# A gating mixer's two dense products by seven block products for eight

## The chip, the cores and the metric

One core of one Trainium2 chip runs the whole program: matrix engine (PE, with its weight loads PEld), vector engine (DVE), scalar engine (ACT), GpSimd (POOL) and the DMA queues, here issued by SP. The metric is the device time of one launch in microseconds, as the median of several runs.

## The reference

Two decoder layers on 1024 positions of width 1024, in float32. Layer 0 mixes tokens by a gating unit, layer 1 by dilated attention; each is followed by a squared-ReLU MLP of width 4096, with RMS norms in front and plain residual adds. The part that is changed:

```python
def _chunk_gating_mixer(h, w_in, ln_g, ln_b, w_s, b_s, w_out):
    uv = jax.nn.gelu(h @ w_in, approximate=False)
    u, v = jnp.split(uv, 2, axis=-1)
    v = _layer_norm(v, ln_g, ln_b)
    v = v.reshape(B_, nc, CHUNK, GATE_GROUPS, GATE_GROUP_DIM)
    w = jnp.where(causal[None], w_s, 0.0)
    mixed = jnp.einsum('gts,bnsgc->bntgc', w, v) + b_s.T[None, None, :, :, None]
    gate = mixed.reshape(B_, S_, GATE_WIDTH)
    return (u * gate) @ w_out
```

with `h = x + mixer(rms_norm(x))`. So there are three dense products here, v, u and the output, each 1024 x 1024 x 1024, and a small causal product inside each chunk of 128 positions.

## The kernel before

Activations lie transposed, channels on the partitions: `h` is eight tiles of 128 channels by 1024 positions, worked on in two halves of 512. A float32 product is made of three passes: every operand is split into a high part (ACT copies it into a rounded type, L208) and a low part (DVE subtracts, L209), and PE does high x high, high x low and low x high. So a block of 128 x 128 weights with 512 columns is three matmuls, and each weight tile costs one ACT and one DVE operation for each 512 columns (`split`, `weight`, `Pair`).

PE's instructions stand in the order in which the program writes them. `Flow` keeps a rough PE clock by which side work (norms, the gate, attention) is woven into that order. The other engines' orders come from a scheduler that ranks by the order of writing and by `tc.high_priority`. An engine takes its queue strictly in order. Tiles come from pools: `wpool` with 8 weight tiles, `slots` with 28 large tiles, `tpool` with 8 temporaries `t`, 4 raw weight tiles `r` and 2 spares `b`; PSUM has 3 banks `mm` and 5 banks `at`. A new tile waits for whoever still uses its buffer.

The mixer runs in this order:

1. The v product, eight chunks of 128 positions in groups of three, three and two (`gi` = 0, 1, 2), over eight depth blocks k; each k needs one split weight pair from `w_v`. While it runs, x is scaled by the norm's gain and split (`scaled`, L456 and L457), and its squares are summed on POOL (`Square`, L264). The RMS factor is applied later: to v in the gelu (L538), to u by `rsb`.
2. `spatial`, woven in for each chunk: statistics, normalising (L511), split, 24 small matmuls against the causal gate weights, and the gate back to SBUF (L525) in place of v in `vg`.
3. The u product, output tile by output tile (`mm`, 24 matmuls for each half), then `u_out`: times `rsb` (L589), gelu (L590), times the gate (L593), and `u_split`.
4. The output product in the same plain form, added to `h` by `add_h` (L308).

The MLPs already use block products by seven (the scheme of Strassen and Winograd): both operands are cut into 2 x 2 blocks, sums of blocks are formed, and seven products give what eight gave. `Weights` loads four raw blocks and `steps` forms the sums on POOL (L351 to L356) and splits the seven operands; `product` runs one of them; `Terms` forms the sums of the normed input; `hidden_terms` those of the hidden activations, which are stored in DRAM and fetched again. `Down` is the MLP's second product: it goes in turns over the depth blocks, adds each product to `h` where it belongs (L830), and keeps the last depth block (`we`, `xe`) as a plain product for the end (`close`), so that the next norm can start by halves.

Of the kernel before, what the change touches and what calls it, by code (L numbers as in the profile page):

```python
# [10 lines left out]
F32 = mybir.dt.float32  # L11
# [101 lines left out]
def trunk(ctx: ExitStack, tc: tile.TileContext, xT, w_u, w_v, w_o, w_s, b_s, w_qkv, w_vt, w_bo, rel,  # L113
# [5 lines left out]
    slots = ctx.enter_context(tc.tile_pool(name="slots", bufs=28))  # L119
    wpool = ctx.enter_context(tc.tile_pool(name="wpool", bufs=8))  # L120
    tpool = ctx.enter_context(tc.tile_pool(name="tpool", bufs=8))
    small = ctx.enter_context(tc.tile_pool(name="small", bufs=4))
# [18 lines left out]
    class Pair:  # L141


        def __init__(self, t):
            self.hi, self.lo = t[:, 0, :], t[:, 1, :]

        def split(self, src):
            n = src.shape[1]
            split(self.hi[:, 0:n], self.lo[:, 0:n], src)
            return self  # L150
# [49 lines left out]
    h = [const.tile([P, S], F32, name=f"h{k}") for k in range(KT)]  # L200
# [6 lines left out]
    def split(hi, lo, src):  # L207
        nc.scalar.activation(hi, src, AF.Copy)  # L208
        nc.vector.tensor_tensor(lo, src, hi.bitcast(F32), op=ALU.subtract)  # L209
# [116 lines left out]
    def product(bank, w, xs, more=False):  # L326

        for k, x in enumerate(xs):
            three(bank, w, blk(k), x, not more and k == 0, k == len(xs) - 1, skip_group_check=True)
            flow.pump()  # L330

    class Weights:
# [10 lines left out]
        def split(self, p, src):  # L343
            self.w[p] = self.place().split(src)
# [104 lines left out]
    def scaled(s, k):  # L449

        x, g = h[k][:, half(s)], vec[:, 0, k:k + 1]
        hi, lo = pair().both()
# [5 lines left out]
        ys[s].append((hi, lo))  # L458
        sq[s].add(k)

# [36 lines left out]
    def spatial():  # L497
        for n in range(8):
            yield v_done[n], 600
            v = vg[n]  # L500
            st = small.tile([P, 2, 6], F32, tag="bn", name="bn")
# [6 lines left out]
            for i in range(2):  # L508
                t, hi, lo = temp(), rtemp(), rtemp()
                c = slice(i * HALF, (i + 1) * HALF)  # L510
                nc.vector.tensor_scalar(t, v[:, c], mv[:, 0:1], r, op0=ALU.subtract, op1=ALU.mult)  # L511
                split(hi, lo, t)
                parts.append((hi, lo))
            yield LAT["gate"]
# [15 lines left out]
    gelus = []  # L530
# [11 lines left out]
    for gi, chunks in enumerate(((0, 1, 2), (3, 4, 5), (6, 7))):  # L542
        banks = {}
        for k in range(KT):
# [7 lines left out]
            with tc.issue_after(roots[0] if k == 1 else gelus[5]) if gi == 1 and k else nullcontext():  # L552
                w = weight(w_v[k])
# [20 lines left out]
            for e, i, n, f in order:  # L574
                x, c = ys[n // 4][k], blk(n % 4)
# [4 lines left out]
                if k == 7 and e == 2 and f == 1:  # L580
# [3 lines left out]
                    else:  # L584
                        v_out(banks, chunks[:i + 1])

    def u_out(m, s, ps):
        t = temp()
        nc.vector.tensor_tensor(t, ps, rsb[:, half(s)], op=ALU.mult)  # L589
        nc.scalar.activation(t, t, AF.Gelu)  # L590
        for b in range(4):
            x = vg[4 * s + b][:, blk(m)]
            nc.vector.tensor_tensor(x, x, t[:, blk(b)], op=ALU.mult)  # L593

    def u_split(s):
        out = []
        for m in range(8):
            hi, lo = pair().both()
            for b in range(4):
                split(hi[:, blk(b)], lo[:, blk(b)], vg[4 * s + b][:, blk(m)])  # L600
            out.append((hi, lo))
        return out

    us = []
    for tiles in ((0, 1, 2), (3,), (4,), (5, 6, 7)):
        w = [weight(w_u[m]) for m in tiles]
        for s in range(2):
            for i, m in enumerate(tiles):
                b = mm_bank()
                mm(b, w[i], KCOLS, ys[s])  # L610
                flow.until(lambda: gated[4 * s + 3].t is not None)
                u_out(m, s, b)
            if tiles[-1] == 7:
                us.append(u_split(s))


    sq = [Square(half(0)), Square(half(1))]
    terms = Terms()
    for tiles in ((0, 1), (2,), (3,), (4, 5, 6, 7)):
        w = [weight(w_o[m]) for m in tiles]  # L620
        for s in range(2):
            for i, m in enumerate(tiles):
                b = mm_bank()
                mm(b, w[i], KCOLS, us[s])
                add_h(m, half(s), b)
                sq[s].add(m)
            if tiles[-1] == 7:
                start_terms(sq[s], s, 1, terms)
                if s == 0:
                    first = [plain(0, q) for q in range(2)]  # L630

# [17 lines left out]
    def hidden_terms(q, c11, c21, c12, c22, t2, store=True):  # L649
# [11 lines left out]
        return {1: c11, 3: c22, 7: t3, 5: c12, 2: c21, 6: t2, 4: t4}  # L661

    def mlp(layer, x, first, last):
# [35 lines left out]
        for q in range(2, 16):  # L699
            down = Down(layer) if q == 15 else None  # L700
# [74 lines left out]
    class Down:  # L775

        def __init__(self, layer):
            self.layer = layer
            self.order = [14, *range(14)]
            self.x = {k: {} for k in self.order}
            self.u = {}
            self.todo = [(t % 4, range(max(0, t - 3), min(t, 14) + 1)) for t in range(18)]

        def weights(self, t, **kw):
            a, ks = self.todo[t]

            runs = []
            for k in (self.order[i] for i in ks):
                if runs and k == runs[-1][1]:
                    runs[-1][1] += 1
                else:
                    runs.append([k, k + 1])
            return Weights(lambda i, j: [w_dn[self.layer, a, i, j][:, lo * P:hi * P] for lo, hi in runs], **kw)

        def take(self, k, src, which):
            for p in which:  # L800
                self.x[k][p] = pair("hx").split(src[p])

        def early(self, which):

            src = {}
            for n, p in enumerate(which):
                if n % 2 == 0:
                    two = slot((P, 2, HALF), F32, "hr")
                src[p] = load(hidden_tile(0, p), two[:, n % 2, :])
            self.take(0, src, which)  # L810

        def inputs(self, t, which):
            k = self.order[t] if t < 15 else 0
            if k:
                self.take(k, {p: load(hidden_tile(k, p), temp()) for p in which}, which)

        def run(self, w):
            for t, (a, ks) in enumerate(self.todo):
                hs = {(i, s): h[a + 4 * i][:, half(s)] for i in range(2) for s in range(2)}
                wn = None  # L820
                if t < 17:
                    wn = self.weights(t + 1, **(dict(own=temp, place=pair) if t == 16 else {}))
                more = ahead(wn)
                more()

                def xs(p):
                    return [self.x[self.order[k]][p] for k in ks]

                def add(i, s, src, engine=nc.vector):
                    return engine.tensor_tensor(hs[i, s], hs[i, s], src, op=ALU.add).ins  # L830

                def then(evacuated, p):

                    with tc.issue_after(evacuated) if t < 3 else nullcontext():
                        more()
                        self.inputs(t + 1, (p,))

                if t == 16:
                    self.ends(0)
                a_ = mm_bank()  # L840
                product(a_, w[1], xs(1))
                if t < 4:
                    self.u[a] = spare() if t < 2 else temp()
                    more()
                    nc.scalar.activation(self.u[a], a_, AF.Copy)
                    self.inputs(t + 1, (1,))
                else:
                    more()
                    nc.vector.tensor_tensor(self.u[a], self.u[a], a_, op=ALU.add)
                    self.inputs(t + 1, (1,))  # L850
                d = at_bank()
                product(d, w[5], xs(5))
                then(add(1, 1, d), 5)
                e = at_bank()
                product(e, w[7], xs(7))
                then(add(1, 1, e), 7)
                if t == 16:
                    self.ends(1)
                b = at_bank()
                product(b, w[6], xs(6))  # L860
                then(nc.vector.tensor_tensor(self.u[a], self.u[a], b, op=ALU.add).ins, 6)
                product(a_, w[2], xs(2), True)
                then(add(0, 0, a_), 2)
                product(d, w[3], xs(3), True)
                then(add(0, 1, d), 3)
                if t >= 14:
# [624 lines left out]
```

## Time and profile before

| | |
|---|---|
| runs | 2171.8 us median of 3 (2170.54 to 2172.2) |
| profiled execution | span 2174.9 us |
| PE busy | 2139.6 us (98%) |
| DVE busy | 1541.6 us (71%) |
| ACT busy | 1086.5 us (50%) |
| POOL busy | 514.3 us (24%) |
| DMA | 253.88 MB, mean 117 GB/s |
| granted PE clock | 0.996 |

The span is that of one profiled execution, and the page has no other time for it. An engine's busy time is the sum of its instructions' durations; a row of a timeline has the start, the duration, the engine, the line, the operation, what it writes and reads, the shape and, in brackets, how long the engine had been idle in front of it and who ended that. Start-to-start times of instructions that follow each other are a little shorter than their durations, since they overlap at the ends.

### The profile page before, as it was taken

Reading aid. Unit: us, or ns where it says so; the run is one execution under the profiler, and the core shown is the slowest. Engines: PE = TensorE matmul, PEld = TensorE weight load, DVE = VectorE, ACT = ScalarE, POOL = GpSimd, SP = SyncE. Lnnn points to the kernel's source line nnn. Section 1 sums busy time; section 2 is a strip of 40 time slices with the busy share of each in tenths; the row PEclk is TensorE's granted clock in tenths of the full one; section 3 lists DMA queues with packets and bytes.
Section 4 is the critical chain, followed back from the end, with each engine's and each line's share of the span. In section 5 each row is a group of like instructions: output and inputs, shape, how many; then the busy total and the mean of one; then the engine's idle time right before and its main releaser. Section 6 shows DMA issues by size and latency. Waiting matters only on the chain.

```text
span 2174.9 us, 30386 instructions
## 1 busy us (share of the span) xinstructions
PE 2139.6 (98%) x10360; PEld 1774.5 (82%) x10360; DVE 1541.6 (71%) x2855; ACT 1086.5 (50%) x2200; POOL 514.3 (24%) x372
## 2 busy tenths in 40 slices
PE   9999999999999999999999999999999999999997
PEld 7888887888878888788888887887788888788886
DVE  7865277766689887771357676758986667988867
ACT  7644145555564443351356464656555556544433
POOL 2000124333234323510000000001443332333335
PEclk9999999999999999999999999999999999999999
DMA  6421104444355443333321222221155443654432
GB/s 214 131 73 49 39 22 166 160 158 150 119 183 186 146 149 107 107 119 135 121 72 58 74 65 55 75 55 30 39 179 160 156 152 118 193 168 145 151 92 97
DMA packets 167680, 253.88 MB, mean 117 GB/s; under 512 B 33642, under 2 KB 59365, under 8 KB 167525
## 3 DMA queue, kind: packets, MB, share of 16 engines
q1 hardware_dynamic: 166768, 250.71, 36.4%
q8 instruction: 81, 1.33, 0.3%
q10 hardware_dynamic: 756, 1.23, 0.2%
q14 instruction: 75, 0.61, 0.1%
HBM read 182.50 MB, written 69.37 MB: 116 GB/s over the span
## 4 chain that ended last, share of the span: by engine, by line
PE 80%; DVE 8%; DMA 5%; ACT 4%; issue 2%; POOL 1%; SPq 1%; DVEq 0%; ACTq 0%; POOLq 0%
PE at L180 40%; PE mm L180 39%; PE at L187 1%; DMA t<-bvec 1%; ACT t L1136 1%; DVE wp L209 1%; DMA sc<-st 1%; DMA h<-in_xT 1%; DMA r<-in_w_dn 1%; DMA t<-in_w_dl 1%; DVE N L1174 1%; DMA hr<-hid 1%; DVE h L308 0%; DVE h L830 0%; DVE wlo L209 0%
## 5 line engine op out<-in xcount | busy, mean ns | idle before, releaser
L208 ACT ACTIVATE wp<-r 128x512 fp32r<-128x512 f32 (+2 forms) x404 | 240.9, 600 | 356.4 <-PE at L180 229.0
L180 PE MATMUL at<-hx,wp 128*128 128x512 f32 x1770 | 412.9, 389 | 1.7 <-DVE h L830 1.7
L180 PE MATMUL mm<-y,whi 128*128 128x512 f32 x1312 | 412.4, 395 | 0.0
L180 PEld LDWEIGHTS at<-hx,wp 128*128 128x128 f32 x1770 | 332.0, 188 | 71.7 <-DVE h L830 2.6
L209 DVE TENSOR_TENSOR wp<-r,wp 128x512 fp32r<-128x512 f32 (+2 forms) x404 | 323.5, 808 | 77.2 <-ACT wp L208 73.7
L180 PE MATMUL at<-t,wp 128*128 128x512 f32 x1344 | 313.9, 389 | 0.0
L180 PEld LDWEIGHTS at<-t,wp 128*128 128x128 f32 x1344 | 252.2, 188 | 52.8 <-DVE t L739 0.4
L264 POOL TENSOR_TENSOR t<-t 128x512 f32<-128x512 f32 (+1 forms) x66 | 84.1, 1274 | 860.6 <-ACT t L259 858.4
L180 PEld LDWEIGHTS mm<-y,whi 128*128 128x128 f32 x1312 | 240.7, 188 | 50.6
L180 PE MATMUL mm<-y,wlo 128*128 128x512 f32 x656 | 256.0, 390 | 0.0
L351 POOL TENSOR_TENSOR t<-r 128x512 f32<-128x512 f32 (+3 forms) x62 | 92.7, 1494 | 596.6 <-DMA r<-in_w_up 194.1
L180 PE MATMUL mm<-y,wp 128*128 128x512 f32 x912 | 222.7, 390 | 0.4 <-DVE y L209 0.2
L180 PEld LDWEIGHTS mm<-y,wp 128*128 128x128 f32 x912 | 170.7, 188 | 37.4 <-issue 0.6
L180 PE MATMUL mm<-hx,wp 128*128 128x512 f32 x708 | 172.6, 390 | 3.2 <-DVE hx L209 1.6
L180 PEld LDWEIGHTS mm<-hx,wp 128*128 128x128 f32 x708 | 132.4, 188 | 32.9 <-DVE hx L209 2.5
L180 PEld LDWEIGHTS mm<-y,wlo 128*128 128x128 f32 x656 | 123.1, 188 | 26.8
L209 DVE TENSOR_TENSOR hx<-t,hx 128x512 fp32r<-128x512 f32 x192 | 141.1, 741 | 1.9 <-ACT hx L208 1.9
L830 DVE TENSOR_TENSOR h<-h,at 128x512 f32<-128x512 f32 x144 | 98.0, 683 | 48.6 <-PE at L180 46.0
L208 ACT ACTIVATE hx<-t 128x512 fp32r<-128x512 f32 x192 | 119.0, 630 | 17.8 <-DMA t<-hid 13.7
L209 DVE TENSOR_TENSOR wlo<-r,whi 128x512 fp32r<-128x512 f32 x138 | 98.9, 735 | 40.8 <-ACT whi L208 35.6
L208 ACT ACTIVATE whi<-r 128x512 fp32r<-128x512 f32 x138 | 84.0, 627 | 84.4 <-PE mm L180 54.3
L180 PE MATMUL at<-y,wp 128*128 128x512 f32 x480 | 119.0, 390 | 0.7 <-DVE wp L209 0.7
(199 smaller groups left out, 3199.8 us busy)
## 6 DMA issues: line engine op xcount, KB each, us to landing
t<-hid SPq DMA_DIRECT2D x182, 256.0 KB, 3.2
hid<-t SPq DMA_DIRECT2D x140, 256.0 KB, 2.3
r<-in_w_up SPq DMA_DIRECT2D x128, 256.0 KB, 2.7
r<-in_w_dn SPq DMA_DIRECT2D x88, 256.0 KB, 2.6
hid<-b SPq DMA_DIRECT2D x56, 256.0 KB, 2.2
r<-in_w_qkv SPq DMA_DIRECT2D x50, 256.0 KB, 2.6
r<-in_w_v SPq DMA_DIRECT2D x48, 256.0 KB, 3.5
vd<-vs SPq DMA_DIRECT2D x16, 512.0 KB, 4.2
```

The source lines that it names most:

```text
L180: nc.tensor.matmul(out, lhsT, rhs, **kw)
L187: nc.tensor.transpose(out, src, ident)
L208: nc.scalar.activation(hi, src, AF.Copy)
L209: nc.vector.tensor_tensor(lo, src, hi.bitcast(F32), op=ALU.subtract)
L264: nc.gpsimd.tensor_tensor(self.acc, self.acc, sq, op=ALU.add)
L351: tt(r3, r[0, 0], r[1, 0], op=ALU.subtract)
L830: return engine.tensor_tensor(hs[i, s], hs[i, s], src, op=ALU.add).ins
L1136: nc.scalar.activation(p[:, c], p[:, c], AF.Exp, bias=m, scale=-1.0, accum_out=dn)
L1174: nc.vector.tensor_tensor(o, o, pv[r, c], op=ALU.add)
```

## The change

The u product becomes four turns of seven products (`gated_product`), with sums of the scaled x formed on POOL (`x_combine`) in place, in the tiles of `h`, and split as terms (`x_terms`). Since this destroys x, it is loaded again (`x_again`) for the residual. In the first turn the products 1, 3 and 2 come first, with banks of their own, because they need no sums of x. u's tiles go through `u_out` (now into a temporary, the gate product 128 columns at a time) and `hidden_terms`, and the terms of the first two turns are stored and fetched.

The output product becomes a `Down` with four depth blocks, the last of them plain as in the MLP. `Down` itself gets a count `n`, and a `side` generator by which the last turn's u tiles are finished between its products. Weights of the first turn are combined ahead and split partly on POOL (`combine`, `parts`). The last group of the v product takes three weight pairs at once, and `spatial` gets a raised priority from the second chunk on. `h` moves into `slots` (now 40); `small` has 3 buffers.

```diff
-    h = [const.tile([P, S], F32, name=f"h{k}") for k in range(KT)]
+    h = [slot(name="h") for k in range(KT)]
...
-    def split(hi, lo, src):
+    def split(hi, lo, src, engine=None):
         nc.scalar.activation(hi, src, AF.Copy)
-        nc.vector.tensor_tensor(lo, src, hi.bitcast(F32), op=ALU.subtract)
+        (engine or nc.vector).tensor_tensor(lo, src, hi.bitcast(F32), op=ALU.subtract)
...
+        def combine(self):
+            r, tt = self.r, nc.gpsimd.tensor_tensor
+            s2, s4, r3 = spare(), spare(), self.own()
+            tt(r3, r[0, 0], r[1, 0], op=ALU.subtract)
+            tt(r[1, 0], r[1, 0], r[1, 1], op=ALU.add)
+            tt(s2, r[1, 0], r[0, 0], op=ALU.subtract)
+            tt(s4, r[0, 1], s2, op=ALU.subtract)
+            self.src = {1: r[0, 0], 3: s4, 2: r[0, 1], 5: r[1, 0], 7: r3, 6: s2, 4: r[1, 1]}
+
+        def parts(self, ps):
+            for p in ps:
+                self.split(p, self.src[p], None if p in (1, 3, 2) else nc.gpsimd)
...
+    def x_combine(k):
+        for o in (k, k + 4):
+            nc.scalar.activation(h[o], h[o], AF.Copy, scale=vec[:, 0, o:o + 1])
+        y = [h[o][:, half(s)] for o in (k, k + 4) for s in range(2)]
+        tt = nc.gpsimd.tensor_tensor
+        tt(y[0], y[1], y[0], op=ALU.subtract)
+        tt(y[1], y[3], y[1], op=ALU.subtract)
+        tt(y[3], y[3], y[0], op=ALU.subtract)
+        tt(y[2], y[2], y[3], op=ALU.subtract)
+
+    def x_terms():
+        for p, k in [(5, k) for k in range(4)] + [(7, k) for k in range(4)] + [(p, k) for k in range(4) for p in (6, 4)]:
+            if (p, k) == (6, 1):
+                yield v_done[7], 0
+            y = h[k if p in (5, 7) else k + 4][:, half(p in (7, 6))]
...
+            xs[p].append(pair("x").split(y, nc.gpsimd if p in (7, 4) else None))
+            yield XT
...
+            quick = tc.high_priority(offset=PRIO // 2) if n > 0 else nullcontext()
...
+                for i in range(3) if k == 0 else range(k + 2, min(k + 3, KT)):
+                    last_w.append(weight(w_v[i]))
+                w = last_w[k]
...
-    def u_out(m, s, ps):
-        t = temp()
-        nc.vector.tensor_tensor(t, ps, rsb[:, half(s)], op=ALU.mult)
+            if gi == 1 and k > 3:
+                with tc.issue_after(gelus[5]):
+                    x_combine(k - 4)
+            if gi == 2 and k == 0:
+                first_u = Weights(lambda i, j: w_u[0, i, j], temp)
+                first_u.combine()
+            if gi == 2 and k == 3:
+                flow.add(x_terms())
+
+    def u_out(q, i, s, src, t=None):
+        m, t = q + 4 * i, temp() if t is None else t
+        flow.until(lambda: gated[4 * s + 3].t is not None)
+        (nc.vector if q == 3 or (i, s) == (0, 0) else nc.gpsimd).tensor_tensor(t, src, rsb[:, half(s)], op=ALU.mult)
         nc.scalar.activation(t, t, AF.Gelu)
         for b in range(4):
-            x = vg[4 * s + b][:, blk(m)]
-            nc.vector.tensor_tensor(x, x, t[:, blk(b)], op=ALU.mult)
-    def u_split(s):
...
-    for tiles in ((0, 1, 2), (3,), (4,), (5, 6, 7)):
-        w = [weight(w_u[m]) for m in tiles]
...
-    for tiles in ((0, 1), (2,), (3,), (4, 5, 6, 7)):
-        w = [weight(w_o[m]) for m in tiles]
...
+            nc.vector.tensor_tensor(t[:, blk(b)], t[:, blk(b)], vg[4 * s + b][:, blk(m)], op=ALU.mult)
+        return t
...
     class Down:
-        def __init__(self, layer):
+        def __init__(self, w, wl, n):
...
+            if n < 4:
+                self.todo = [(0, range(2)), (1, range(3)), (2, range(3)), (3, range(3)), (0, range(2, 3))]
+                self.fetch = {1: 1}
...
+    def x_again(a):
+        for o in (a, a + 4) if a < 4 else ():
+            h[o] = slot(name="h")
+            nc.sync.dma_start(h[o], xT[blk(o)])
+
+    def gated_product():
+        w = first_u
+        w.parts((1, 3, 2, 5, 7, 6, 4))
+        late = []
+        for q in range(4):
+            down = Down(w_on, w_ol, 3) if q == 3 else None
+            wn = down.weights(0) if down else Weights(lambda i, j: w_u[q + 1, i, j])
+            more = ahead(wn)
...
+            a = mm_bank()
+            product(a, w[1], xs[1], n=4)
...
+            u = temp()
+            nc.scalar.activation(u, a, AF.Copy)
+            if q == 0:
+                d2 = mm_bank()
+                product(d2, w[3], xs[3], n=4)
+                a2 = mm_bank()
+                product(a2, w[2], xs[2], n=4)
+                c11 = temp()
+                nc.vector.tensor_tensor(c11, u, a2, op=ALU.add)
+                u_out(q, 0, 0, c11, c11)
+            if down:
+                down.take(2, held, SEVEN[:4])
+            d = at_bank()
+            product(d, w[5], xs[5], n=4)
...
+            if q > 0:
+                product(a, w[2], xs[2], True, 4)
+                more()
+                c11 = u_out(q, 0, 0, a)
+                product(d, w[3], xs[3], True, 4)
+                more()
+                c12 = temp()
+                nc.vector.tensor_tensor(c12, u, d, op=ALU.add)
+                if q < 3:
+                    u_out(q, 0, 1, c12, c12)
+            product(e, w[4], xs[4], True, 4)
...
+        def left():
+            cs = {(1, 1): c22, (0, 1): c12, (1, 0): c21, (0, 0): c11}
...
+        down.run(w, left())
+        down.close([(half(s), begin_mlp) for s in range(2)])
```

More of the change, by code (lines that the diff above doesn't have):

```diff
@@ L897, in trunk, with begin_mlp @@
+    terms, first = Terms(), []
+    def begin_mlp(sq):
+        start_terms(sq, sq.cols.start // HALF, 1, terms)
+        if not first:
+            first.extend(plain(0, q) for q in range(2))
+    gated_product()
     tab = small.tile([33, 24], F32, name="tab", bufs=1)
```

356 lines of the change are left out of this document (208 added, 148 removed).

## The prediction

> **What bounds the kernel now.** First the page: its span and the engines' busy time.
>
> ```profile
> span 2174.9 us, 30386 instructions
> PE 2139.6 (98%) x10360; PEld 1774.5 (82%) x10360; DVE 1541.6 (71%) x2855; ACT 1086.5 (50%) x2200; POOL 514.3 (24%) x372
> ```
>
> The matrix engine (PE) is idle for 35.3 us in all. The span is 3.1 us above the median of the runs (2171.8), so I work out a difference against the span and add it to the median. Next the chain that ended last: it gives what one matmul costs, and where the u product starts (114.39, behind the last value matmul).
>
> ```profile
> 114.39 8.85 PE mm L180 x39
> 142.35 2.63 PE at L180 x24
> 144.98 134.07 PE mm L180 x591
> ```
>
> 591 matmuls of 512 columns in 134.07 us are 0.227 us each; 24 small ones of the gate (128 columns) take 2.63, or 0.11 each. Then the windows around the start of the u product, with one from the down product for later:
>
> ```profile
> 88.00:114.40 26.40, 26.40 (x144) 22.70 (x142) 22.39 (x59) 18.73 (x32) 0.00 (x0) 1.00 0.46 140
> 114.40:145.00 30.60, 30.60 (x172) 26.58 (x172) 23.63 (x74) 13.39 (x22) 0.00 (x0) 1.00 0.12 38
> 641.00:690.00 49.00, 48.10 (x212) 39.50 (x212) 47.55 (x64) 26.24 (x46) 19.75 (x14) 1.00 0.59 186
> ```
>
> The columns are PE, weight loads, DVE, ACT, POOL. PE is full in both stages. DVE is already busy for 22.4 of 26.4 and 23.6 of 30.6 us, and POOL does nothing there. The change puts work into just these two places.
>
> **What is removed.** The u product falls from 384 matmuls to 4 turns x 7 products x 4 blocks x 3 passes = 336. The output product does only three of its four depth blocks by seven: 252, and 96 for the last as before, so 348 instead of 384. That is 84 fewer (not the 96 that "seven for eight" would give): 84 x 0.227 = **19.1 us**. PE is the bound on both sides of the change, so all of it counts unless PE now waits.
>
> **What is added, first block of the u product.** The seven products need sums of x. x_combine does 16 subtractions on POOL and 8 wide scalings on ACT; 16 x terms are split, half on POOL; u_out multiplies 9 tiles by rsb on POOL; the recombination adds four to six DVE operations to a turn. What does a POOL operation cost DVE? From the timelines of both in one turn of the first MLP:
>
> ```profile
> 423.55 1.67 DVE L653 TENSOR_TENSOR t<-t 128x512 f32<-128x512 f32 x1
> 425.14 0.68 DVE L763 TENSOR_TENSOR t<-t,at 128x512 f32<-128x512 f32 x1
> 425.73 1.18 DVE L209 TENSOR_TENSOR wp<-r,wp 128x512 fp32r<-128x512 f32 x1
> 427.61 1.61 DVE L658 TENSOR_TENSOR b<-t 128x512 f32<-128x512 f32 x1
> 429.14 1.28 DVE L209 TENSOR_TENSOR wp<-r,wp 128x512 fp32r<-128x512 f32 x2
> 423.01 1.66 POOL L351 TENSOR_TENSOR t<-r 128x512 f32<-128x512 f32 x1 [10.38 <-DVE wp L209]
> 424.75 1.62 POOL L352 TENSOR_TENSOR r<-r 128x512 f32<-128x512 f32 x1
> 427.06 1.61 POOL L353 TENSOR_TENSOR r<-r 128x512 f32<-128x512 f32 x1 [0.69 <-DVE wp L209]
> 429.96 1.62 POOL L356 TENSOR_TENSOR r<-r 128x512 f32<-128x512 f32 x1 [1.28 <-issue]
> 291.59 1.29 POOL L264 TENSOR_TENSOR t<-t 128x512 f32<-128x512 f32 x1 [6.32 <-ACT t L259]
> ```
>
> A DVE operation with both inputs in SBUF that starts inside a POOL operation ends 0.55 us after it: 1.67, 1.18 and 1.61 instead of 0.69. The one that reads PSUM (425.14) takes its 0.68 beside POOL. Four POOL operations cost DVE 0.98 + 0.49 + 0.92 + 0 = 2.4 us, **0.6 each**. The Trainium skill states this as a rule ("SBUF — State Buffer", Who interferes with whom): GpSimd and a Vector operation with two SBUF inputs exclude each other for the whole instruction, and one with a single SBUF input is free; by that rule, the trace agrees (0.68 at 425.14). By the rule alone, an estimate is POOL's undisturbed 1.29 us times the half of DVE's work that takes two SBUF inputs, 0.65 for 0.6, and a sum 1.3 us higher.
>
> How much DVE has to do follows from the changed program's order and these starts:
>
> ```profile
> 82.68 0.69 DVE L503 BATCH_NORM_STATS2 bn<-vg 128x6 f32<-128x512 f32 x1 [1.31 <-ACT vg L538]
> 88.12 1.11 DVE L525 SCALAR_TENSOR_TENSOR vg<-at,vec,rb 128x128 f32<-128x128 f32 x4
> 89.15 0.14 DVE L240 TENSOR_SCALAR rv<-mv 128x1 f32<-128x1 f32 x1
> 89.99 0.55 DVE L511 TENSOR_SCALAR t<-vg,mv,rq 128x512 f32<-128x512 f32 x1
> 92.22 0.54 DVE L511 TENSOR_SCALAR t<-vg,mv,rq 128x512 f32<-128x512 f32 x1
> 92.68 0.69 DVE L503 BATCH_NORM_STATS2 bn<-vg 128x6 f32<-128x512 f32 x1
> 93.29 0.67 DVE L209 TENSOR_TENSOR wlo<-r,whi 128x512 fp32r<-128x512 f32 x1
> 147.08 2.51 DVE L209 TENSOR_TENSOR y<-vg,y 128x128 fp32r<-128x128 f32 x12
> 662.54 0.68 DVE L209 TENSOR_TENSOR wp<-r,wp 128x512 fp32r<-128x512 f32 x1
> 663.14 0.68 DVE L209 TENSOR_TENSOR hx<-t,hx 128x512 fp32r<-128x512 f32 x1
> 65.37 1.14 ACT L208 ACTIVATE whi<-r 128x512 fp32r<-128x512 f32 x2
> ```
>
> From start to start: 0.60 for a 512-column operation, 0.61 for statistics, 0.46 for the normalising step, 0.21 for 128 columns from SBUF, 0.26 for 128 from PSUM, 0.12 for a one-column one (seven from 89.15 to 89.99). At 82.68 DVE had waited 1.31 us for a gelu, so it carries no backlog. From there to the last operand that the gate of chunk 7 needs, the changed order holds 49, 10, 10, 14, 42 and 35 of these kinds: 29.4 + 6.1 + 4.6 + 2.9 + 10.9 + 4.2 = 58.1 us. Until 93 it can't run ahead, since the gelus of the second group come one by one: it does some 4.5 us of this in the first 10.3, so 5.7 are lost. DVE is there at 82.7 + 63.8 = 146.5, if POOL costs nothing.
>
> PE gets there after 84 + 12 + 12 large and 60 small matmuls behind 114.4: 24.5 + 6.6, so 145.5. DVE is 1.0 late before POOL counts. POOL runs 42 operations from x_combine's first to this point. By an estimate, from a start near 67, 11 lie before 82.7, where DVE had slack, six beside the 5.7 us of waiting, and 25 fall on a full DVE queue: 25 x 0.6 = 15.0. The eight wide scalings stand ahead of the second group's gelus on ACT, 8 x 1.14 us (the last row: two halves), most of it in ACT's pauses; I take 1.5. Together PE waits **17.5 us**, in pieces: at the last value weights, at the first weights of turn 1, at the gate of chunk 7. With 0.35 and 0.9 us for a POOL operation it is 11.3 and 25.0. POOL's splits and multiplications are of a form that the trace lacks; I price them as its subtractions.
>
> Behind that point DVE has time: to the last output turn but one, 70 us of work and some 13 of POOL's blocking against 91 us of matmuls.
>
> **What is added, output product.** It takes over the down product's form, and with it the places where PE waits there. At its start and its end, in the first MLP, and its start in the second:
>
> ```profile
> 616.80 0.97 PE L180 MATMUL mm<-hx,wp 128*128 128x512 f32 x3 [0.24 <-ACT b L845]
> 630.46 0.73 PE L180 MATMUL mm<-hx,wp 128*128 128x512 f32 x2 [0.20 <-DVE hx L209]
> 637.51 2.34 PE L180 MATMUL mm<-hx,wp 128*128 128x512 f32 x9 [0.17 <-ACT t L845]
> 642.78 2.33 PE L180 MATMUL at<-hx,wp 128*128 128x512 f32 x9 [0.90 <-DVE h L830]
> 902.47 1.12 PE L180 MATMUL mm<-hx,y 128*128 128x512 f32 x3 [2.35 <-DVE b L849]
> 914.85 6.41 PE L180 MATMUL mm<-xe,we 128*128 128x512 f32 x27 [0.28 <-DVE h L308]
> 921.87 1.05 PE L180 MATMUL at<-ones,t 128*128 128x1 f32 x8 [0.61 <-DVE t L268]
> 933.38 0.96 PE L180 MATMUL mm<-wp,y 128*128 128x512 f32 x3 [1.01 <-DVE h L308]
> 1848.99 0.96 PE L180 MATMUL mm<-hx,wp 128*128 128x512 f32 x3 [0.89 <-ACT b L845]
> 1863.85 0.73 PE L180 MATMUL mm<-hx,wp 128*128 128x512 f32 x2 [1.41 <-DVE hx L209]
> 1876.16 2.33 PE L180 MATMUL at<-hx,wp 128*128 128x512 f32 x9 [0.83 <-DVE h L830]
> ```
>
> The start costs 1.5 or 3.1 us; I take 2.3. The end costs 4.2 (2.35 + 0.28 + 0.61 + 1.01), and here too the last turn is 21 matmuls and the closing one 96, so 4.2; at least 0.6, if only the norm's wait stays. The one-by-one products before have no such waits.
>
> The second load of x (4 MB) and the new stores and loads go through SP, with DMA 0.12 busy in 114 to 145: nothing, while each is asked for a turn ahead. A store that waits for its DVE result holds the next weights behind it on SP; they too are a turn early. A u_out gelu that waits for POOL holds weight copies behind it on ACT, and so DVE's low parts; that is part of the 17.5.
>
> **The sum:** -19.1 + 17.5 + 2.3 + 4.2 = **+4.9 us**: 2179.8 for a profiled span, 2176.7 for a run; I say 2177. With the ends of the terms: -19.1 + 11.3 + 1.5 + 0.6 = -5.7 and -19.1 + 25.0 + 3.1 + 4.2 = +13.2, so 2166 to 2185 in this case.
>
> **The rivals.** *Faster: the blocking is hidden.* If a POOL operation costs DVE under about 0.2 us in the first block, because POOL's run falls beside PSUM-fed operations (27 of the 58 us of DVE work there take no second SBUF input) and beside waits, then the first block loses 1.0 + 1.5 + 25 x 0.2 = 7.5 at most, 2.5 at least; with 2.3 and 2 at the output product that gives -12 to -7, about 2162. For it: PE lost only 0.9 us in 641 to 690, where DVE was 47.6 of 49 us busy beside 19.8 of POOL. Against it: there each turn's weights had been split during the turn before, and here nothing is ahead, since the value weights hold the buffers. The sum changes its sign at 0.4 us for a POOL operation. *Much slower:* the first output turn has 42 matmuls (9.5 us) and DVE some 15.5 us of splits and sums around it; if DVE arrives there without a lead, 6 us more are lost, and with the 0.9 price that gives 2188 to 2192. The Trainium skill ("TensorE: Matmul & The Clock Gate", What's actually happening) says that the clock halves behind an idle window of 3.4 us; no wait here is that long (2.35 at most, the clock 1.00). *Less than announced:* that 84 and not 96 matmuls go is in the sum.
>
> **How the numbers follow.** The first case has 0.62, the faster rival 0.26, the much slower one 0.12. About 0.2% (4.3 us) is what a measurement can tell from no change. Of the first case, 0.04 lies below -4.3, 0.19 within, 0.39 above. So faster 0.30, same 0.19, slower 0.51. The range reaches down to the middle of the faster rival and just over the top of the first case: 2162 to 2187; alone the likeliest case has 2166 to 2185.
>
> **What would show it.** Right: PE idle grows by over 15 us between 88 and 170 us, ended by DVE (wlo, wp, tr), with DVE operations of 1.2 to 1.8 us beside POOL; the DVE queue without a pause from 93 to 160; 84 matmuls fewer; some 4 us at the end of the output product. Wrong: PE idle under 10 us in that stretch (then the faster rival), or most of the waiting in the output product, or a later MLP that is not as long as now.

## The result, and the profile after

The changed kernel takes 2205.5 us (median of 5 runs, 2204.1 to 2208.9) against 2171.8 before. The ratio is 1.0158, with a 95% interval of 1.0146 to 1.0171: it is 1.6% slower, where I had forecast 2177 with a range up to 2187. The sign was right; the loss is over six times as large. Its page, first lines:

```profile
span 2205.3 us, 30394 instructions
PE 2140.3 (97%) x10276; PEld 1768.9 (80%) x10276; DVE 1635.5 (74%) x2911; ACT 1112.1 (50%) x2232; POOL 627.3 (28%) x458
```

84 matmuls fewer, as worked out (10276 for 10360), and yet PE is as busy as before (2140.3 for 2139.6 us). The windows say why. First those of the kernel after (span of the window, then PE, weight loads, DVE, ACT, POOL, the granted clock, DMA share, GB/s):

```profile
45.00:88.00 43.00, 36.59 (x166) 29.23 (x167) 41.47 (x71) 28.04 (x46) 24.30 (x16) 0.88 0.22 74
88.00:114.40 26.40, 23.78 (x115) 19.96 (x114) 22.63 (x61) 22.85 (x34) 4.53 (x3) 0.87 0.50 162
114.40:145.00 30.60, 24.04 (x109) 20.05 (x109) 27.83 (x47) 17.70 (x33) 20.48 (x14) 0.83 0.20 59
170.00:200.00 30.00, 24.69 (x103) 20.49 (x102) 23.38 (x55) 8.11 (x14) 10.16 (x8) 0.83 0.26 97
250.00:300.00 50.00, 43.38 (x178) 34.93 (x177) 47.24 (x76) 22.55 (x49) 22.26 (x19) 0.93 0.54 173
45.00:300.00 255.00, 223.37 (x994) 182.28 (x995) 230.73 (x434) 134.83 (x239) 117.75 (x83) 0.91 0.35 113
```

And the last of these of the kernel before:

```profile
45.00:300.00 255.00, 253.89 (x1225) 212.90 (x1225) 156.61 (x426) 114.72 (x232) 21.63 (x15) 1.00 0.22 68
```

From 45 to 300 us, PE idles for 31.6 us instead of 1.1, DVE is busy for 231 of 255 us instead of 157, and the clock is 0.91 instead of 1.00. In windows of 2 us, the clock's loss while PE is busy adds up to 16.9 us. So: -19.1 for the matmuls, +30.5 idle, +16.9 half clock is +28.3. The span grew by 30.4. Idle time and clock in the rest of the program are 2.5 us better than before; the 4.6 us that are then missing I put down, without a test, to the lead-out of each interrupted row of matmuls (a single one after a wait shows 0.50 us, where 0.227 is its share in a row), some twenty times. The waits of PE that matter most below (in brackets the idle time in front and who ended it):

```profile
70.18 0.50 PE L180 MATMUL at<-wlo,y 128*128 128x512 f32 x1 [1.87 <-DVE wlo L209]
73.84 0.80 PE L180 MATMUL at<-wlo,y 128*128 128x512 f32 x1 [2.37 <-DVE wlo L209]
98.53 0.48 PE L180 MATMUL at<-wsh,tr 128*128 128x128 f32 x1 [1.89 <-ACT vg L583]
135.73 0.69 PE L180 MATMUL at<-wsh,tr 128*128 128x128 f32 x2 [6.40 <-DVE tr L209]
162.18 3.01 PE L180 MATMUL at<-x,wp 128*128 128x512 f32 x12 [0.83 <-DVE t L979]
176.80 0.47 PE L180 MATMUL at<-wsh,tr 128*128 128x128 f32 x1 [3.42 <-ACT tr L208]
248.78 1.64 PE L180 MATMUL at<-hx,wp 128*128 128x512 f32 x6 [1.55 <-DVE h L748]
266.85 2.37 PE L180 MATMUL at<-hx,wp 128*128 128x512 f32 x9 [2.83 <-DVE h L748]
283.22 7.11 PE L180 MATMUL at<-hx,wp 128*128 128x512 f32 x18 [3.79 <-DVE h L748]
```

They begin at 70 us, in the v product, and end with the output product. The one of chunk 7 (176.80) isn't of DVE's making. Chunk 7 had been normalised at 152.6, but its split stands in ACT's queue behind a gelu of the u product, as the timelines of DVE, POOL and ACT show:

```profile
151.60 1.00 DVE L554 TENSOR_SCALAR vg<-vg,mv,rq 128x512 f32<-128x512 f32 x2
173.55 0.67 DVE L1012 TENSOR_TENSOR t<-t,at 128x512 f32<-128x512 f32 x1
174.30 1.26 POOL L651 TENSOR_TENSOR t<-t,rsb 128x512 f32<-128x512 f32 x1 [1.03 <-DVE t L1012]
175.60 0.63 ACT L652 ACTIVATE t<-t 128x512 f32<-128x512 f32 x1 [4.86 <-POOL t L651]
176.14 0.61 ACT L208 ACTIVATE tr<-vg 128x512 fp32r<-128x512 f32 x1
```

PE's last matmul in front of the wait ends at 173.38. DVE adds its result to a sum, POOL multiplies it by rsb, ACT takes the gelu, and only then comes the split that PE waits for. With the two short waits behind it this place costs 5.2 us of idle time and 4.0 of half clock. No run moved the split ahead of the gelu.

Now DVE in the v product, beside x_combine:

```profile
77.20 1.65 DVE L209 TENSOR_TENSOR wlo<-r,whi 128x512 fp32r<-128x512 f32 x1
78.78 0.14 DVE L240 TENSOR_SCALAR rv<-mv 128x1 f32<-128x1 f32 x1
78.84 1.72 DVE L209 TENSOR_TENSOR wlo<-r,whi 128x512 fp32r<-128x512 f32 x1
80.56 1.69 DVE L209 TENSOR_TENSOR wlo<-r,whi 128x512 fp32r<-128x512 f32 x1
82.17 1.25 DVE L244 TENSOR_TENSOR ra<-rr,rv 128x1 f32<-128x1 f32 x1
84.82 1.93 DVE L554 TENSOR_SCALAR vg<-vg,mv,rq 128x512 f32<-128x512 f32 x2
105.81 1.00 DVE L554 TENSOR_SCALAR vg<-vg,mv,rq 128x512 f32<-128x512 f32 x2
```

And POOL in the same stretch:

```profile
78.27 1.74 POOL L486 TENSOR_TENSOR h<-h 128x512 f32<-128x512 f32 x1
79.97 1.73 POOL L484 TENSOR_TENSOR h<-h 128x512 f32<-128x512 f32 x1
81.78 1.62 POOL L485 TENSOR_TENSOR h<-h 128x512 f32<-128x512 f32 x1
```

The two take turns: one DVE instruction to one of POOL, each 1.6 to 1.7 us from start to end. Small ones with two inputs in SBUF aren't spared: the one-column product at 82.17 takes 1.25 us instead of 0.16, and the two normalising steps at 84.82 together 1.93, where the same pair takes 1.00 at 105.81 with POOL idle.

**A ledger of DVE.** I count DVE's instructions from 57.5 us to the last operand of chunk 7's gate, each with its undisturbed time from start to start (those of the prediction, 0.60 for 512 columns and so on): that is its own work. Gaps between instructions are its pauses. What is left of the stretch is the time for which instructions were held. The kernels *sums left out*, *block on DVE* and *fillers* are those of the next section.

| kernel | stretch | own work | pauses | held | POOL operations | held per operation |
|---|---|---|---|---|---|---|
| before | 57.5 to 143 | 67.7 | 16.0 | 1.8 | 1 | |
| after | 57.5 to 182 | 80.9 | 9.5 | 34.1 | 47 | 0.73 |
| sums left out | 57.5 to 172 | 82.2 | 10.6 | 21.7 | 31 | 0.70 |
| block on DVE | 57.5 to 171 | 98.6 | 6.0 | 8.9 | 14 | 0.64 |
| fillers | 57.5 to 186 | 82.9 | 9.9 | 35.7 | 47 | 0.76 |

DVE is done with the first block 39 us later than before: 13.2 more work of its own, 32.3 held by POOL, 6.5 fewer pauses. The last operand of chunk 7 comes by the chain above, so the end of the stretch isn't set by DVE's queue alone.

### The profile page after: what moved, and what is told of

It is laid out like the page before. It is cut to its first block, busy times and chain, and to the rows that moved or that the text cites. A ratio compares the mean times of both kernels' runs of the same rounds, so it can differ in the third digit from the quotient of the medians.

```text
span 2205.3 us, 30394 instructions
## 1 busy us (share of the span) xinstructions
PE 2140.3 (97%) x10276; PEld 1768.9 (80%) x10276; DVE 1635.5 (74%) x2911; ACT 1112.1 (50%) x2232; POOL 627.3 (28%) x458
## 4 chain that ended last, share of the span: by engine, by line
PE 75%; DVE 10%; ACT 4%; DMA 4%; issue 3%; POOL 2%; SPq 0%; DVEq 0%; POOLq 0%; ACTq 0%
PE at L180 41%; PE mm L180 32%; PE at L187 2%; DVE wp L209 1%; DVE wlo L209 1%; DMA r<-in_w_v 1%; DMA h<-in_xT 1%; DMA t<-bvec 1%; ACT t L1295 1%; DVE h L308 1%; DVE t L654 1%; DVE tr L209 1%; ACT whi L208 1%; DMA r<-in_w_dn 1%; DVE h L748 0%
## 5 line engine op out<-in xcount | busy, mean ns | idle before, releaser
L180 PE MATMUL at<-hx,wp 128*128 128x512 f32 x1935 | 455.4, 391 | 10.2 <-DVE h L748 10.2
L208 ACT ACTIVATE wp<-r 128x512 fp32r<-128x512 f32 (+2 forms) x446 | 262.3, 593 | 366.3 <-PE at L180 236.3
L180 PEld LDWEIGHTS at<-hx,wp 128*128 128x128 f32 x1935 | 364.4, 189 | 89.2 <-DVE h L748 12.7
L180 PE MATMUL mm<-y,whi 128*128 128x512 f32 x800 | 254.1, 399 | 0.0
L180 PE MATMUL mm<-y,wp 128*128 128x512 f32 x1020 | 249.2, 391 | 0.6 <-DVE y L209 0.2
L209 DVE TENSOR_TENSOR hx<-t,hx 128x512 fp32r<-128x512 f32 x204 | 177.0, 889 | 18.6 <-ACT hx L208 18.4
L180 PEld LDWEIGHTS mm<-y,whi 128*128 128x128 f32 x800 | 145.1, 188 | 31.0
L180 PE MATMUL mm<-y,wlo 128*128 128x512 f32 x400 | 156.3, 391 | 0.0
L371 POOL TENSOR_TENSOR r<-r 128x512 f32<-128x512 f32 (+3 forms) x69 | 102.9, 1491 | 72.5 <-issue 59.3
L180 PEld LDWEIGHTS at<-y,wp 128*128 128x128 f32 x516 | 96.6, 188 | 22.8 <-issue 1.3
```

The source lines that it names most:

```text
L180: nc.tensor.matmul(out, lhsT, rhs, **kw)
L209: (engine or nc.vector).tensor_tensor(lo, src, hi.bitcast(F32), op=ALU.subtract)
L371: tt(r[0, 0], r[0, 1], r[1, 1], op=ALU.subtract)
```

## The experiments

The times of different chips differ by some us, so ratios to the kernel before, run beside each, are compared; the changed kernel's is 1.0158. A is my theory: the first block is set by DVE's queue, and POOL's operations fill it by holding DVE.

**All POOL work of the first block done by DVE** (block_dve; the first pair of lines stands for x_combine and for `combine`):

```diff
-        tt = nc.gpsimd.tensor_tensor
+        tt = nc.vector.tensor_tensor
-                self.split(p, self.src[p], None if p in (1, 3, 2) else nc.gpsimd)
+                self.split(p, self.src[p])
-                nc.gpsimd.tensor_copy(t, y)
+                nc.vector.tensor_copy(t, y)
-            xs[p].append(pair("x").split(y, nc.gpsimd if p in (7, 4) else None))
+            xs[p].append(pair("x").split(y))
```

> 33 POOL operations of the first block (the 16 sums of x, the 4 sums of the first weights, 4 of their splits, 8 splits of x terms, one copy) are done by DVE in 0.60 us each, so DVE gets 20 us more work of its own. Theory A (a POOL operation holds DVE for about 1.0 us, whole alternation): DVE loses 33 us of being held and gains 20, so it is some 13 us earlier; the waits of 70 to 182 us shrink and with them the stretches of half clock: 2188 to 2196 us. Rival B (DVE simply has too many operations and is held for at most 0.2 us): 13 us later, about 2218 us. The prediction's own price of 0.6 us: no difference, 2205 us.

Measured: 1.0107 (1.0092 to 1.0122), 2198.3 us: 11 us less than the changed kernel. By the ledger DVE does 17.7 us more, is held for 25.2 less (0.76 for each of the 33 operations) and pauses for 3.5 less: 11.0 us, and it is done with the block at 171 instead of 182 us. So an operation of POOL costs more here than the same operation on DVE itself (0.60); at the price of 0.6 there would be no gain, at 0.2 a loss. Of the second group's waits for weights 0.37 and 0.84 us are left, though the one for the gate's bank is longer (3.44 us at 92.42 for 1.89 at 98.53). The wait at chunk 4's gate is 2.59 us instead of 6.40. And 23 us remain to the kernel before: between 45 and 201 us PE still idles for 15.4 us and loses 10.4 by half clock. That DVE has too much work there even without POOL is one reading, argued and not shown, for the chain at chunk 7's gate stands in this run too: its gelu waits 4.88 us for a product that was left on POOL.

**The sums of x left out** (no_sums; the four subtractions of x_combine are struck out):

> The 16 sums of x are left out (the scaled x itself is split as terms, so the u product has other numbers); all else stays. Theory A: the waits of the second group of the v product (1.87 and 2.37 us at 70 and 74 us, 1.89 at 98.5) and the half clock behind them (2.1 and 3.0 us of matmul time) go, and DVE comes to the first turn earlier: 2188 to 2196 us. Rival B (volume, not blocking): DVE's queue is the same, so at most 3 us: 2202 us or more.

Measured: 1.0099 (1.0083 to 1.0114), 13 us less than the changed kernel. DVE's own work is much the same (82.2 us for 80.9), and it is held for 12.4 us less. The wait at chunk 4's gate shows the shift plainly. In this kernel's timeline of PE:

```profile
124.07 0.69 PE L180 MATMUL at<-wsh,tr 128*128 128x128 f32 x2 [6.40 <-DVE tr L209]
```

The same wait, 6.40 us, ends at 124.07 instead of 135.73: everything came 11.7 us earlier, and the waiting behind it stayed. That speaks against volume alone, for there no DVE instruction is saved.

**Fillers** (matmuls of zeros in front of four waits, so that PE doesn't rest):

```diff
+    def fill(bank, rhs, n):
+        for _ in range(n):
+            nc.tensor.matmul(bank[0:32], zero, rhs, start=False, stop=False, skip_group_check=True)
...
+                if (gi, k, e, i) == (1, 4, 2, 0):
+                    fill(banks[n, f], w[0][:, half(f)], 8)
...
+                    if (n, i, g) == (4, 1, 0):
+                        fill(o, wsh[:, 0, :], 48)
```

> All of the computation stays; PE gets matmuls that add zeros or are overwritten, at four places where it waits: 2 x 8 (0.227 us each) at the two waits of 70 to 74 us, 48 small ones at the wait of 6.40 us before 135.7, 14 before 176.8, 14 before 283.2. They do nothing but keep PE at work. If the clock halves because PE waited, and its loss comes on top of the waits (theory A): the half clock behind these four places goes, 2.1 + 3.3 + 3.9 + 2.9 = 12.2 us of matmul time, so 2193 to 2197 us. Rival C (DVE sets the end there, so that PE at full clock only waits longer): 2203 to 2208 us, with the clock at 1.00 all the same.

Measured: 1.0180 (1.0165 to 1.0195), no less than the changed kernel and perhaps 5 us more, and also a little over rival C's range. Between 45 and 300 us the loss by half clock fell from 16.9 to 8.1 us and idle time from 31.6 to 24.6, but a wait of 3.18 us had only moved behind 300, to 302.74. Between 45 and 341 us the loss by half clock is 11.0 instead of 16.9 us and idle time 28.0 instead of 32.3: 10 us less, and the fillers themselves take some 15 by their count. In this kernel's timeline of PE:

```profile
136.39 0.44 PE L180 MATMUL at<-wsh,tr 128*128 128x128 f32 x2 [3.56 <-DVE tr L209]
163.85 4.37 PE L180 MATMUL at<-x,wp 128*128 128x512 f32 x12 [3.33 <-DVE t L994]
```

Chunk 4's operand comes at 136.39 (135.73 in the changed kernel), and at the next wait PE arrives 0.8 us earlier and waits for 3.33 us where it waited for 0.83. So at these two places the clock isn't a loss beside the others: DVE sets when things come, and a PE that is quicker waits longer. My theory had added the half clock to the waits; that part fell here. What the half clock alone costs stays open, since a filler takes PE's time as well.

**Only the output product by seven** (u_plain): the u product is plain, x is not destroyed.

```diff
-            if gi == 1 and k > 3:
-                with tc.issue_after(gelus[5]):
-                    x_combine(k - 4)
...
+        def u_plain(q, w, s):
+            for i in range(2):
+                b = mm_bank()
+                for k in range(KT):
+                    three(b, w[i, k // 4], blk(k % 4), ys[s][k], k == 0, k == KT - 1)
...
+                nc.vector.tensor_tensor(t, b, rsb[:, half(s)], op=ALU.mult)
```

> The u product is plain again (96 matmuls for each pair of output tiles, no sums of x, no second load of x); only the output product goes by seven: 36 matmuls fewer than before, so 2171.8 - 8.2 = 2163.6 us if nothing else. Theory A: the first block has no waits; if the waits of the output product (1.22 + 1.55 + 2.83 + 3.79 us, and 2.9 of half clock) belong to the form of Down, 2174 to 2178 us; if they come from the u turn's gate products, sums and the reloading in between, 2164 to 2169 us. Rival D (the output product is what costs): over 2185 us.

Measured: 0.9987 (0.9978 to 0.9997), 3 us less than the kernel before. In its timeline the output product has one wait of note:

```profile
269.80 0.93 PE L180 MATMUL mm<-hx,y 128*128 128x512 f32 x3 [1.21 <-DVE b L758]
```

No wait at its start, no half clock. So the form of Down costs 1.2 us here, and the u product by seven carries nearly all of the loss, with what it leaves over for the output product. Of the 8.2 us that 36 matmuls are worth, 2.0 go at the start: the first gelus come later (PE's wait there ends at 45.66 instead of 43.62 us, and at 45.95 in the changed kernel). With the 1.2 that leaves 5 us, where 3 were measured; the other 2 are open.

**With the second load of x** (u_reload), and **with the reload asked for earlier** in the changed kernel (reload_early):

```diff
-            plan = {2: (x_again, 1), 8: (out, 1, 1), 9: (x_again, 2), 10: (out, 0, 1), 12: (out, 1, 0), 14: (keep, 0, 0),
-                    15: (keep, 1, 1), 16: (x_again, 3), 17: (keep, 0, 1), 19: (keep, 1, 0)}
+            plan = {0: (x_again, 1), 8: (out, 1, 1), 4: (x_again, 2), 10: (out, 0, 1), 12: (out, 1, 0), 14: (keep, 0, 0),
+                    15: (keep, 1, 1), 11: (x_again, 3), 17: (keep, 0, 1), 19: (keep, 1, 0)}
```

> The kernel with the plain u product and the output product by seven (ratio 0.9987), with x loaded a second time for the residual at the same places as in the changed kernel. If the reload is what makes the output product wait (theory E), waits of 3 to 9 us come back in it: a ratio of 1.000 to 1.003. If it is the side work of the last u turn (rival F), the ratio stays at 0.998 to 0.9995 and the output product has one wait of 1.2 us as without the reload.

Measured: 0.9989 (0.9980 to 0.9998), as without the reload. Loading x twice costs nothing by itself.

> As the changed kernel, but three of the four second loads of x are asked for 2, 5 and 5 steps of the side work earlier. The changed kernel took 1.0158 of the time before. Theory E: in the output product the additions that empty PSUM stand behind gate products and splits on DVE, because they are placed where the reloaded h is expected; with h there earlier they are placed earlier, and of the waits of 1.55, 2.83 and 3.79 us and the 2.9 us of half clock 5 to 9 us go: a ratio of 1.0115 to 1.0135. Rival F (DVE has too much side work there, in whatever order): 1.015 to 1.017.

Measured: 1.0139 (1.0126 to 1.0153), some 4 us less than the changed kernel, less than theory E said and more than its rival. The wait of 2.83 us is gone, that of 3.79 is 2.89; that at the start is 1.80 for 1.55, one of 1.30 is new, and 3.4 us of half clock remain. With u_reload beside it, the likeliest reading is that the reload's place matters through the order that the scheduler makes of it; no run changed that order alone. What stood in DVE's queue ahead of the late addition, in the changed kernel:

```profile
275.07 3.61 DVE L654 TENSOR_TENSOR t<-t,vg 128x128 f32<-128x128 f32 x4
278.61 0.68 DVE L209 TENSOR_TENSOR xe<-t,xe 128x512 fp32r<-128x512 f32 x1
279.21 1.35 DVE L209 TENSOR_TENSOR wp<-r,wp 128x384 fp32r<-128x384 f32 x1
280.49 2.08 DVE L209 TENSOR_TENSOR xe<-t,xe 128x512 fp32r<-128x512 f32 x2
282.49 0.68 DVE L748 TENSOR_TENSOR h<-h,at 128x512 f32<-128x512 f32 x1
```

Four gate products take 3.61 us instead of 0.89, for POOL adds to h beside them from 272.58 to 276.30, and the addition that frees PE's bank comes last.

**The last turn's side work left out** (no_side; `out` in `left` does nothing):

> The changed kernel without the factor, gelu and gate product of the last three u tiles, which it does as side work during the output product (the sums are split as they are, so the output has other numbers). Theory F (this side work on DVE and POOL is what keeps the additions that empty PSUM back): of the waits of 2.83 and 3.79 us and the half clock of 2.9 us 6 to 9 us go: a ratio of 1.0117 to 1.013. If the waits belong to Down's form or to the reload: 1.0145 to 1.017.

Measured: 1.0133 (1.0118 to 1.0149), some 5 us less than the changed kernel, just past the weak end of theory F. From 250 to 300 us PE now idles for 2.2 us and the clock stays at 1.00; the waits of 2.83 and 3.79 us are gone. Those at the start (1.31 and 1.45) stay. So the side work is what the two longer waits and the half clock come from, and not the two at the start.

**The same dose of POOL work in two places of the kernel before** (dose_early, dose_late): 16 subtractions that nobody needs.

```diff
+    def pool_dose(k):
+        dead = spare()
+        for o in (k, k, k + 4, k + 4):
+            nc.gpsimd.tensor_tensor(dead, h[o][:, half(1)], h[o][:, half(0)], op=ALU.subtract)
```

> The kernel before, with 16 additional POOL subtractions of 512 columns, whose results nobody reads, at the place where the changed kernel forms its sums of x (from about 57 us on). Theory A: they hold DVE for 0.8 us each, 12.8 us, where DVE has 2.4 us of pauses up to 83 us; PE waits 4 to 8 us for value weights and loses 2 to 4 us by half clock, and DVE catches up behind it (12 us of pauses to 143 us): a ratio of 1.003 to 1.0055. As the prediction counted (11 of 16 in pauses, 0.6 us for the others): 3 us of DVE that are caught up: at most 1.001.

> The kernel before, with the same 16 additional POOL subtractions, tied to output tiles 3 and 4 of the u product (about 140 to 190 us), where DVE is idle for almost half of the time. Theory A: they hold DVE just as long and nobody waits for it: a ratio of 0.999 to 1.001, with no new wait of PE. If POOL's work costs in itself (a slower PE, ACT or DMA): 1.002 or more in both places.

Measured: early 1.0070 (1.0057 to 1.0082), 15 us; late 0.9996 (0.9987 to 1.0005), nothing. The early dose ran even sooner than I had placed it, from 38 to 63 us, beside the norm's root and the first gelus. Its windows, and PE's and POOL's timelines:

```profile
45.00:88.00 43.00, 35.48 (x149) 29.68 (x150) 39.91 (x82) 22.79 (x40) 22.90 (x16) 0.80 0.27 86
```

```profile
47.15 1.22 PE L180 MATMUL at<-whi,y 128*128 128x512 f32 x2 [3.81 <-ACT vg L543]
64.50 0.80 PE L180 MATMUL at<-wlo,y 128*128 128x512 f32 x1 [4.95 <-DVE wlo L209]
```

```profile
46.32 16.52 POOL L449 TENSOR_TENSOR b<-h 128x512 f32<-128x512 f32 x12
```

Two waits make 7.7 us of idle time from 45 to 300 us (1.1 without the dose), and 7.5 us of half clock lie behind them: together 14.1 of the 15. From 88 us on PE is full again. That is more than theory A had said, whose place for the dose was 57 us. Here DVE has 16.7 us of pauses between 83 and 150 us and holds PE up no more, and the loss by the clock comes in full on top of the waits, unlike at the two places of the fillers. The late dose, POOL and DVE, with DVE's own row without POOL in front:

```profile
161.21 12.04 POOL L449 TENSOR_TENSOR b<-t,h 128x512 f32<-128x512 f32 x8 [93.88 <-ACT t L595]
173.45 12.04 POOL L449 TENSOR_TENSOR b<-t,h 128x512 f32<-128x512 f32 x8 [0.19 <-ACT t L595]
```

```profile
150.71 0.89 DVE L598 TENSOR_TENSOR vg<-vg,t 128x128 f32<-128x128 f32 x4
169.03 3.07 DVE L598 TENSOR_TENSOR vg<-vg,t 128x128 f32<-128x128 f32 x4
```

From 160 to 186 us it holds DVE for 12.1 us, 0.76 for each operation, as much as anywhere; but DVE was idle for almost half of this time, and nobody waits. The same work costs 15 us in one place and none in the other.

**A version that beats both** (u_hconst): the output product by seven, u plain, and h in tiles of its own (with `slots` at 32 instead of 40).

```diff
-    h = [slot(name="h") for k in range(KT)]
+    h = [const.tile([P, S], F32, name=f"h{k}") for k in range(KT)]
```

> The kernel with the plain u product and the output product by seven, with h in tiles of its own as before instead of in the common pool. Theory G: h in the pool alters the order of the first loads of x and of the value weights, which costs the 2.0 us by which the first gelus come later (PE's wait ends at 45.66 instead of 43.62): a ratio of 0.9975 to 0.998. Rival: the 2 us come from the raised priority of the normalising work or from the three buffers, which stay: 0.9985 to 0.999.

Measured: 0.9972 (0.9962 to 0.9983), 6 us less than before. The wait at the first gelus ends at 43.16 us, so theory G holds: with h in the pool, the scheduler had put single value-weight loads ahead of x's. A last try put the evacuations of Down's last turns first (u_best; `tc.high_priority` around them):

> The former kernel, and in the last two turns of every Down the additions that empty PSUM go ahead on DVE. It takes away the wait of 1.21 us at the end of the output product, those of 2.22 and 1.4 us at the ends of the two MLPs' second products and the half clock behind the first of these (1.7 us): 4 to 6 us less than the former kernel, a ratio of 0.995 to 0.9965. If the additions were not what PE waited for: no difference to the former.

Measured: 0.9968 (0.9956 to 0.9981), no more than u_hconst. The waits that it was to take away are still there (1.20 in the output product, 2.42 at the end of the first MLP's): in the timeline they stand where they stood, so the raised rank didn't move these additions to the front. What would is open.

## Why the prediction was right and wrong

*Matmuls.* 84 fewer, as worked out, and the kernel slower: right.

*The first block.* The term of 17.5 us was the one that was too small: between 45 and 201 us PE idles for 21.7 us, against 0.9 before, and loses 14.0 by half clock, for which the sum had nothing.

*The price of a POOL operation* (0.6): low, but not the main error. The ledgers give 0.64 to 0.76, and 34.1 us for the changed kernel.

*"11 lie before 82.7, where DVE had slack": this is the step that failed first.* The count was right, though x_combine starts at 61, not near 67: 11 of its operations and three squares lie before 82.2. The slack was not there: in the kernel before, DVE has 2.4 us of pauses in that stretch, no more. I had read "waited 1.31 us for a gelu" at 82.68 as slack for all that lay before. By the ledger from 57.5 to 82.2, DVE was held for 11.8 us and did 12.9 us of its own work instead of 20.4. From 82.2 on it therefore had 68.8 us to do where I had counted 58.1, with 9.5 us of pauses (counted: 5.7) and 21.9 held by 33 operations (counted: 25 operations, 15.0; six more were to fall into waiting). That adds up to 21 us that the prediction didn't have, and moves the end of the block to 182 instead of 161.5. Of these, 7.5 us are the backlog from before 82.2. The 16 sums themselves are worth 13 us of the kernel's time, as the run without them shows.

*The row of PE's waits.* "PE idle grows by over 15 us between 88 and 170" came out as 10.0, but 6.4 us lie before 88 and 5.3 behind 170; the stretch was drawn by the same error. DVE's rows of 1.2 to 1.8 us beside POOL, and the releasers wlo and tr, were as said. A DVE queue "without a pause from 93 to 160" was not: it paused for 7.4 us there. "A u_out gelu that waits for POOL holds weight copies behind it on ACT" came true in a worse place, in front of chunk 7's split.

*The output product.* I took 2.3 us at its start and 4.2 at its end, from the MLPs' rows. It cost 9.4 us of waits (1.22, 1.55, 2.83 and 3.79) and 2.9 of half clock at the start and in the middle, and 0.6 at the end. The MLPs' Down has no such side work. u_plain shows that the form by itself costs 1.2 us here, and no_side that the waits of 2.83 and 3.79 us and the half clock come from this work. The two at the start stay without it; they are gone only where the u product is plain, and what in it makes them is open. The second load of x was rightly counted at nothing (u_reload), but for the order that it led to.

*The clock.* "No wait here is that long (2.35 at most, the clock 1.00)" was wrong by the trace that I had, and so the sum lacked a term that came to 16.9 us. In the windows of the kernel before, right behind its wait of 2.35 us:

```profile
904.00:906.00 2.00, 2.00 (x7) 1.47 (x6) 2.00 (x4) 0.63 (x1) 1.09 (x1) 0.50 0.33 126
```

*The rivals.* Hidden blocking needed under 0.2 us for a POOL operation; the changed kernel's ledger has 0.73. "Much slower" had the right sign and wrong mechanism: it put the loss in the first output turn, and it stopped at 2192.

## What to carry to other kernels

Before work is given to an engine that "does nothing there", make the ledger of the engine that shares with it, stretch by stretch: own work, pauses, and what the new operations hold. One pause at the end of a stretch isn't slack for the stretch. Move such work to where the held engine is idle for half of its time: 16 operations cost 15 us in one place and nothing a hundred us later. Where another engine sets when operands come, fewer matmuls and a better clock on PE gained nothing here: the wait grew instead. And follow a wait past the engine that its row names: the 3.42 us at chunk 7's gate were no lack of DVE's time, but a split that stood behind a gelu in ACT's queue.

## What I had not expected of the hardware

A one-column DVE product with two inputs in SBUF is held as long as a wide one (1.25 us for 0.16), and the normalising step, which reads one wide tile, is held too (0.97 each for 0.50). The Trainium skill ("SBUF — State Buffer", Who interferes with whom) lets an operation with one input in SBUF pass, outside modes of two ports, and names tensor_scalar among those that can enter such a mode. The first half agrees with the one-column operation at 78.78, which takes its 0.14 us inside POOL's operation from 78.27 to 80.01. I had only read that half; the normalising step fits the second, but no run here shows in which mode it works.

PE's clock halves behind much shorter waits than I took for the limit: in the changed kernel from about 98 us on, inside a wait of 1.89 us with small matmuls in front of it, and not behind the wait of 2.83 us that ends at 266.85 (clock 1.00 from 264 to 272). A stretch of half clock lasts 3.4, 6.8 or 10.2 us by the trace's clock record, matmuls 0.43 us apart. Up to 300 us the stretches begin at 46.74, 70.64, 97.94, 132.08, 176.45 and 282.26 us, each a whole number of 3.413 us after the first. On this grid the wait of 2.83 us is cut into 1.17 and 1.66, while 2.83 us of the wait of 3.79 and 3.07 of that of 3.42 fall into the one window just in front of their stretch. How much idle time is enough doesn't come out of these traces. The Trainium skill ("TensorE: Matmul & The Clock Gate", What's actually happening) speaks of free-running windows of 3.4 us, and of one idle window as the condition. The grid and stretches of one to three windows fit these traces; that a whole window must be idle does not.
